# Narrower tiles toward the end, and the final combine moved to GpSimd, in a row-variance kernel

## The chip, the cores and the metric

The kernel runs on one core of one Trainium2 chip. The metric is the device time of one execution in microseconds (us). A kernel's *span* in the profile is 1.7 to 1.9 us shorter than the measured time of the same execution; I call that difference "outside".

## The reference

For each of 32 x 512 rows of 1024 floats: the mean of the squares minus the square of the mean.

```python
x = np.random.randn(32, 512, 1024).astype(np.float32)
mean_sq = np.mean(x**2, axis=-1)
sq_mean = np.mean(x, axis=-1)**2
return (mean_sq - sq_mean).astype(np.float32)
```

It reads 67 MB and writes 64 KB. The 16384 rows lie on 128 partitions, so each partition holds 128 rows. I call row *c* of all partitions together a *column*: 128 x 1024 floats, 0.5 MB.

## The kernel before

It loads 16 tiles of 8 columns (4 MB each) into 4 buffers. In each tile one column goes to the variance instructions of VectorE ("bn"), the other seven are *split*: VectorE sums them in one reduction, ScalarE squares them one by one and accumulates the sum of squares. Then ScalarE squares the mean (`mean_sq`), and VectorE does the final subtraction.

```python
io_pool = tile_pool(name="io", bufs=4);  as_pool = tile_pool(name="ascratch", bufs=2)
NBN = 1;  NSPLIT = 7                      # RPP = 8 columns per tile
for n in range(ntiles):                   # 16
    x_tile = io_pool.tile([P, RPP, D], fp32)
    nc.sync.dma_start(out=x_tile, in_=x_all[n])
    # ... bn_stats, bn_stats, bn_aggr of column 0; GpSimd copies its variance into res_all
    nc.vector.reduce_sum(out=sum_x, in_=x_tile[:, NBN:RPP, :], axis=X)
    act_scratch = as_pool.tile([P, D], fp32)          # one scratch per tile
    for j in range(NSPLIT):
        nc.scalar.activation(out=act_scratch, in_=x_tile[:, NBN + j, :],
                             func=SQ, accum_out=sum_sq[:, j : j + 1])
    nc.scalar.activation(out=mean_sq, in_=sum_x, func=SQ, scale=inv_d)
    nc.vector.scalar_tensor_tensor(out=res_all[...], in0=sum_sq, scalar=inv_d,
                                   in1=mean_sq, op0=mult, op1=subtract)
nc.sync.dma_start(out=out_v, in_=res_all)
```

## Time and profile before

| | before |
|---|---|
| measured time, median | 173.24 us (173.32 with the later runs) |
| span | 171.7 us (of an execution that took 173.46) |
| first tile taken up / last tile taken up | 13.53 / 159.93 us |
| last result written / output transfer issued | 169.18 / 169.25 us |

From the page of the kernel before: busy time of each engine, then the span in 40 slices, each digit the busy share in tenths.

```profile
DVE 145.4 (85%) x80; ACT 133.3 (78%) x241; POOL 3.2 (2%) x20
...
DVE  0008989898998989898998989899897989899893
ACT  2008969696988969696987969697895969698792
...
DMA  6999999999999999999999999999999999997000
```

The DMA row is full until slice 36, partly busy in slice 37 and then empty, while VectorE (DVE) and ScalarE (ACT) work on for three slices. That is the exposed end. The windows view of the kernel before gives, for two stretches, the length, the busy time of VectorE, ScalarE and GpSimd (POOL) with the number of instructions, the TensorE clock (not used here), the DMA share and the rate in GB/s:

```profile
20.00:80.00 60.00, 56.21 (x31) 51.15 (x94) 1.11 (x6) 1.00 1.00 432
138.00:156.00 18.00, 16.75 (x11) 15.13 (x28) 0.37 (x2) 1.00 1.00 430
```

The DMA engines are busy all the time at 430 to 432 GB/s: the load stream sets the pace, 1.22 us per column. The timeline of the kernel before, last tile (start, length, engine, line, operation, and in brackets the idle time before it and what ended it):

```profile
159.93 1.06 ACT L70 ACTIVATE act_scratch<-x_tile 128x1024 f32<-128x1024 f32 x1 [0.65 <-DMA x_tile<-in_x_dram]
159.93 0.70 DVE L55 BATCH_NORM_STATS2 stats<-x_tile 128x6 f32<-128x512 f32 x1 [0.45 <-DMA x_tile<-in_x_dram]
...
161.10 1.06 ACT L70 ACTIVATE act_scratch<-x_tile 128x1024 f32<-128x1024 f32 x1
161.13 7.60 DVE L63 TENSOR_REDUCE sum_x<-x_tile 128x7 f32<-128x7168 f32 x1
...
168.76 0.21 ACT L78 ACTIVATE mean_sq<-sum_x 128x7 f32<-128x7 f32 x1 [0.61 <-DVE sum_x L63]
...
169.01 0.17 DVE L80 SCALAR_TENSOR_TENSOR res_all<-sum_sq,mean_sq 128x7 f32<-128x7 f32 x1 [0.16 <-ACT mean_sq L78]
169.25 0.35 SPq L89 DMA_DIRECT2D out_dram<-res_all  x1
```

Nothing of the 9.25 us from 159.93 to 169.18 overlaps with loading. Note the starts of ScalarE's squares, 159.93 and 161.10. Within a tile all 96 such distances in this trace are 1.17 to 1.19 us, mostly 1.18.

### The profile page before, as it was taken

To read this page: it belongs to the slowest core of one execution; us is meant where nothing else is said; L and a number is where in the kernel's file an instruction comes from. 1 tells how busy PE (TensorE), PEld (TensorE's weight loads), DVE (VectorE), ACT (ScalarE), POOL (GpSimd) and SP (SyncE) were. 2 spreads that over 40 slices of the span, in tenths; PEclk is the share of its full clock that TensorE was granted. 3 is DMA by queue.
4 is the path that set the end of the run, shared out by engine and by line. 5 is a ranking of instruction groups with operands and counts; after the bars stand their busy time and mean duration, and the time that the engine had idled before them with its cause. 6 is when DMAs were issued, how large, how long until landed. Compare 5 with 4: busy or idle time off the path is not lost.

```text
span 171.7 us, 425 instructions
## 1 busy us (share of the span) xinstructions
DVE 145.4 (85%) x80; ACT 133.3 (78%) x241; POOL 3.2 (2%) x20
## 2 busy tenths in 40 slices
DVE  0008989898998989898998989899897989899893
ACT  2008969696988969696987969697895969698792
POOL 0000000000000000000000000000000000000000
DMA  6999999999999999999999999999999999997000
GB/s 199 428 435 428 450 420 443 443 420 443 414 435 420 443 435 435 428 443 443 412 443 420 435 428 435 420 443 437 420 437 435 428 435 435 428 428 321 0 0 15
DMA packets 2451, 67.20 MB, mean 391 GB/s; under 512 B 272, under 2 KB 400, under 8 KB 400
## 3 DMA queue, kind: packets, MB, share of 16 engines
q1 hardware_dynamic: 2448, 67.18, 91.4%
q14 instruction: 3, 0.02, 0.0%
HBM read 67.11 MB, written 0.07 MB: 391 GB/s over the span
## 4 chain that ended last, share of the span: by engine, by line
DMA 76%; DVE 21%; SPq 1%; issue 0%; ACT 0%
DMA x_tile<-in_x_dram 76%; DVE sum_x L63 18%; DVE stats L55 2%; DVE stats L56 1%; SPq L48 1%; ACT mean_sq L78 0%; DVE res_all L80 0%
## 5 line engine op out<-in xcount | busy, mean ns | idle before, releaser
L70 ACT ACTIVATE act_scratch<-x_tile 128x1024 f32<-128x1024 f32 x112 | 118.3, 1056 | 25.2 <-DMA x_tile<-in_x_dram 22.2
L63 DVE TENSOR_REDUCE sum_x<-x_tile 128x7 f32<-128x7168 f32 x16 | 121.6, 7601 | 0.0
L55 DVE BATCH_NORM_STATS2 stats<-x_tile 128x6 f32<-128x512 f32 x16 | 11.1, 694 | 21.2 <-DMA x_tile<-in_x_dram 21.2
L70 ACT ACTIVATION_READ_ACCUMULATOR act_scratch<-x_tile 128x1 f32 x112 | 20.8, 186 | 0.0
L78 ACT ACTIVATE mean_sq<-sum_x 128x7 f32<-128x7 f32 x16 | 3.3, 208 | 9.7 <-DVE sum_x L63 9.7
L56 DVE BATCH_NORM_STATS2 stats<-x_tile 128x6 f32<-128x512 f32 x16 | 10.8, 676 | 0.0
L58 POOL COPY res_all<-mv 128x1 f32<-128x1 f32 x16 | 3.0, 185 | 165.7 <-DVE mv L57 165.7
L80 DVE SCALAR_TENSOR_TENSOR res_all<-sum_sq,mean_sq 128x7 f32<-128x7 f32 x16 | 2.7, 167 | 2.5 <-ACT mean_sq L78 2.5
L57 DVE BATCH_NORM_AGGREGATE mv<-stats 128x2 f32<-128x12 f32 x16 | 3.2, 198 | 0.0
L70 ACT ACT_TABLE_LOAD x1 | 1.3, 1283 | 0.7 <-PEq L104 0.7
L104 POOL MEMSET const-float32-0.0<- 128x1 f32 x1 | 0.1, 99 | 0.2 <-issue 0.2
L104 POOL MEMSET const-bfloat16-1.0<- 128x1 bf16 x1 | 0.1, 102 | 0.0
L104 POOL MEMSET const-uint8-127<- 128x1 uint8 x1 | 0.1, 102 | 0.0
L104 POOL MEMSET const-float32-1.0<- 128x1 f32 x1 | 0.1, 99 | 0.0
## 6 DMA issues: line engine op xcount, KB each, us to landing
x_tile<-in_x_dram SPq DMA_DIRECT2D x16, 4096.0 KB, 30.0
out_dram<-res_all SPq DMA_DIRECT2D x1, 64.0 KB, 1.6
```

The lines of the kernel that those rows point to most:

```text
L48: nc.sync.dma_start(out=x_tile, in_=x_all[n])
L55: nc.vector.bn_stats(out=stats[:, j, 0], in_=x_tile[:, j, 0 : D // 2])
L56: nc.vector.bn_stats(out=stats[:, j, 1], in_=x_tile[:, j, D // 2 : D])
L57: nc.vector.bn_aggr(out=mv[:, j], in_=stats[:, j])
L58: nc.gpsimd.tensor_copy(out=res_all[:, c0 + j : c0 + j + 1], in_=mv[:, j, 1:2])
L63: nc.vector.reduce_sum(out=sum_x, in_=x_tile[:, NBN:RPP, :], axis=mybir.AxisListType.X)
L70: nc.scalar.activation(out=act_scratch, in_=x_tile[:, NBN + j, :], func=SQ, accum_out=sum_sq[:, j : j + 1],)
L78: nc.scalar.activation(out=mean_sq, in_=sum_x, func=SQ, scale=inv_d)
L80: nc.vector.scalar_tensor_tensor(out=res_all[:, c0 + NBN : c0 + RPP], in0=sum_sq, scalar=inv_d, in1=mean_sq, op0=mybir.AluOpType.mult, op1 ...
L104: nc = _bacc.Bacc("TRN2", target_bir_lowering=False, num_devices=1)
```

## The change

The intent is to shorten the exposed end. The tiles become narrow: eight of 8 columns, eleven of 4, nine of 2, two of 1. The combine goes to GpSimd in three small operations. There are five load buffers instead of four, three scratches for the squares instead of two, six buffers for the small tiles (sums, squares, results between) instead of four, and four of the 8-column tiles take two bn columns, while six of the 4-column tiles and all narrower ones take none. The diff is shortened.

```diff
-    RPP = 8; ntiles = N // (P * RPP); NBN = 1
+    sched = []
+    for i in range(4):
+        sched += [(8, 2), (8, 1)]                 # (columns, bn columns)
+    for i in range(5):
+        sched += [(4, 0), (4, 1)]
+    sched += [(4, 0)] + [(2, 0)] * 9 + [(1, 0)] * 2
-    io_pool bufs=4;  ascratch bufs=2;  small bufs=4
+    io_pool bufs=5;  ascratch bufs=3;  small bufs=6
     ...
+                    scale=inv_sqrt_d,             # in the square: msq is the mean of squares
-        nc.scalar.activation(out=mean_sq, in_=sum_x, func=SQ, scale=inv_d)
-        nc.vector.scalar_tensor_tensor(out=res_all[...], in0=sum_sq, scalar=inv_d,
-                                       in1=mean_sq, op0=mult, op1=subtract)
+            nc.gpsimd.tensor_tensor(out=t, in0=sum_x, in1=sum_x, op=mult)
+            nc.gpsimd.tensor_scalar(out=t2, in0=t, scalar1=inv_d2, op0=mult)
+            nc.gpsimd.tensor_tensor(out=res_all[...], in0=msq, in1=t2, op=subtract)
```

More of the change, by code (lines that the diff above doesn't have):

```diff
@@ L22 @@
     N = B * S
-    RPP = 8
-    W = RPP * D
-    ntiles = N // (P * RPP)
     C = N // P
     inv_d = 1.0 / D
-    x_all = x.rearrange("b s d -> (b s d)").rearrange(
-        "(p n w) -> n p w", p=P, n=ntiles, w=W
-    )
+    inv_d2 = inv_d * inv_d
+    inv_sqrt_d = float(D) ** -0.5
+    sched = []
[4 more added lines that the diff above has]
+    sched += [(4, 0)] + [(2, 0)] * 9 + [(1, 0)] * 2
+    assert sum(w for w, _ in sched) == C
+    x_cols = x.rearrange("b s d -> (b s d)").rearrange("(p c d) -> p c d", p=P, c=C)
     out_v = out.rearrange("b s -> (b s)").rearrange("(p c) -> p c", p=P)
-    io_pool = ctx.enter_context(tc.tile_pool(name="io", bufs=4))
-    as_pool = ctx.enter_context(tc.tile_pool(name="ascratch", bufs=2))
-    small = ctx.enter_context(tc.tile_pool(name="small", bufs=4))
+    io_pool = ctx.enter_context(tc.tile_pool(name="io", bufs=5))
+    as_pool = ctx.enter_context(tc.tile_pool(name="ascratch", bufs=3))
+    small = ctx.enter_context(tc.tile_pool(name="small", bufs=6))
     res_pool = ctx.enter_context(tc.tile_pool(name="res", bufs=1))
@@ L42 @@
     SQ = mybir.ActivationFunctionType.Square
-    NBN = 1
-    NSPLIT = RPP - NBN
-    for n in range(ntiles):
-        x_tile = io_pool.tile([P, RPP, D], fp32)
-        nc.sync.dma_start(out=x_tile, in_=x_all[n])
-        c0 = n * RPP
-        stats = small.tile([P, NBN, 2, 6], fp32)
-        mv = small.tile([P, NBN, 2], fp32)
-        for j in range(NBN):
-            nc.vector.bn_stats(out=stats[:, j, 0], in_=x_tile[:, j, 0 : D // 2])
-            nc.vector.bn_stats(out=stats[:, j, 1], in_=x_tile[:, j, D // 2 : D])
-            nc.vector.bn_aggr(out=mv[:, j], in_=stats[:, j])
+    MAXW = max(w for w, _ in sched)
@@ new lines @@
+    flush_after = {128: (0, 128)}
+    c0 = 0
+    for n, (w, nbn) in enumerate(sched):
+        x_tile = io_pool.tile([P, MAXW, D], fp32, name="x_tile")
+        nc.sync.dma_start(out=x_tile[:, :w, :], in_=x_cols[:, c0 : c0 + w, :])
+        nsplit = w - nbn
+        if nbn:
+            stats = small.tile([P, 2, 2, 6], fp32, name="stats")
+            mv = small.tile([P, 2, 2], fp32, name="mv")
+            for j in range(nbn):
+                nc.vector.bn_stats(out=stats[:, j, 0], in_=x_tile[:, j, 0 : D // 2])
+                nc.vector.bn_stats(out=stats[:, j, 1], in_=x_tile[:, j, D // 2 : D])
+                nc.vector.bn_aggr(out=mv[:, j], in_=stats[:, j])
@@ L58 @@
             nc.gpsimd.tensor_copy(
-                out=res_all[:, c0 + j : c0 + j + 1], in_=mv[:, j, 1:2]
+                out=res_all[:, c0 : c0 + nbn], in_=mv[:, 0:nbn, 1]
             )
-        sum_x = small.tile([P, NSPLIT], fp32)
-        nc.vector.reduce_sum(
-            out=sum_x, in_=x_tile[:, NBN:RPP, :], axis=mybir.AxisListType.X
-        )
-        sum_sq = small.tile([P, NSPLIT], fp32)
-        act_scratch = as_pool.tile([P, D], fp32)
-        for j in range(NSPLIT):
-            nc.scalar.activation(
-                out=act_scratch,
-                in_=x_tile[:, NBN + j, :],
-                func=SQ,
-                accum_out=sum_sq[:, j : j + 1],
-            )
@@ L77 @@
-        mean_sq = small.tile([P, NSPLIT], fp32)
-        nc.scalar.activation(out=mean_sq, in_=sum_x, func=SQ, scale=inv_d)
-        nc.vector.scalar_tensor_tensor(
-            out=res_all[:, c0 + NBN : c0 + RPP],
-            in0=sum_sq,
-            scalar=inv_d,
-            in1=mean_sq,
-            op0=mybir.AluOpType.mult,
-            op1=mybir.AluOpType.subtract,
-        )
-    nc.sync.dma_start(out=out_v, in_=res_all)
+        if nsplit:
+            sum_x = small.tile([P, MAXW], fp32, name="sum_x")
+            nc.vector.reduce_sum(
+                out=sum_x[:, :nsplit],
+                in_=x_tile[:, nbn:w, :],
+                axis=mybir.AxisListType.X,
+            )
+            msq = small.tile([P, MAXW], fp32, name="msq")
+            act_scratch = as_pool.tile([P, D], fp32)
+            for j in range(nsplit):
+                nc.scalar.activation(
+                    out=act_scratch,
+                    in_=x_tile[:, nbn + j, :],
+                    func=SQ,
+                    scale=inv_sqrt_d,
+                    accum_out=msq[:, j : j + 1],
+                )
+            t = small.tile([P, MAXW], fp32, name="t")
+            nc.gpsimd.tensor_tensor(
+                out=t[:, :nsplit],
+                in0=sum_x[:, :nsplit],
+                in1=sum_x[:, :nsplit],
+                op=mybir.AluOpType.mult,
+            )
+            t2 = small.tile([P, MAXW], fp32, name="t2")
+            nc.gpsimd.tensor_scalar(
+                out=t2[:, :nsplit],
+                in0=t[:, :nsplit],
+                scalar1=inv_d2,
+                scalar2=None,
+                op0=mybir.AluOpType.mult,
+            )
+            nc.gpsimd.tensor_tensor(
+                out=res_all[:, c0 + nbn : c0 + w],
+                in0=msq[:, :nsplit],
+                in1=t2[:, :nsplit],
+                op=mybir.AluOpType.subtract,
+            )
@@ L93 @@
+        c0 += w
+        if c0 in flush_after:
+            lo, hi = flush_after[c0]
+            nc.sync.dma_start(out=out_v[:, lo:hi], in_=res_all[:, lo:hi])
 _INS = ['x']
```

## The prediction

> **What bounds it now.** The load stream. The windows view shows the DMA engines 100% busy at 430 to 433 GB/s from 20 to 140 us. The Trainium skill ("DMA: Bandwidth & Descriptors", Specifications) gives 435 GB/s as the fabric ceiling; the trace agrees. Tiles of eight columns (4 MB) land every 9.71 us typically, 9.76 on average: 1.22 us per column. VectorE (85% busy) and ScalarE (78%) wait for each tile. Exposed is the end: the timeline shows the last tile starting at 159.93; its work ends at 169.18, 9.25 us later, and the output transfer ends the span at 171.7 (2.5 us). The measured 173.24 is 1.5 above the span.
>
> **What changes.** The same bytes in 30 loads instead of 16: eight of 8 columns, eleven of 4, nine of 2, two of 1. The combine moves to GpSimd; `mean_sq` leaves ScalarE. ScalarE takes 116 squares instead of 112, none skipped in the last 24 columns.
>
> **Costs, from the trace.** A ScalarE square starts every 1.18 us (1.056 plus the accumulator read). A reduced VectorE column is 7.60/7 = 1.09 us, a bn column about 1.2. GpSimd's 128x1 copy took 0.185 us; I estimate 0.2 to 0.3 for each of its three small operations. 4 MB at 435 GB/s would be 9.64 us against 9.71, so a load's own overhead is some 0.08 us (estimate): 14 more loads add 1 us of stream.
>
> **The naive gain** is: last load lands near 161, then 1.25 us for one square, 0.3 for the subtract, 2.5 output, 1.5 outside: 166.5.
>
> **I expect less, because ScalarE arrives late.** In the last 24 columns it squares every column at 1.18 us against 1.22 to 1.26 for arrival, so it hardly gains on the stream. When the last 4-column tile lands (column 108: 13.5 + 100 x 1.22 + 0.5 = 136.0) it has a 4.7 us block to do while the following 2-column tile lands after 2.5 us. That lag of over 2 us then shrinks by only about 0.1 us per tile. ScalarE ends at 136.0 + 24 x 1.18 = 164.3, some 3.3 us after the last landing instead of 1.25. Adding 0.3 for the subtract and 2.5 for the output: span 167.1, time 168.7. VectorE at 1.09 per column catches up by the last tiles and does not matter. Five buffers suffice: the lag is two small tiles.
>
> **Predicted: 168.7 us, range 167.2 to 170.3.** Faster by over 2% (below 169.8): 0.78; within 2%: 0.21; slower: 0.01.
>
> **What would show it right.** The DMA row stays at nines until about 160 with 420 GB/s or more in the narrow tiles. In the last 28 us ScalarE has no idle gaps, back to back at 1.18 us, with loads landed before it asks. The chain of waits ends with output, GpSimd subtract, a run of ScalarE squares of about 28 us, and before that DMA. VectorE waits for DMA at the end, ScalarE does not.
>
> **What would make it wrong.**
> - Narrow rows (8 KB and 4 KB per partition instead of 32 KB) stream more slowly: then the last landing moves past about 163 and DMA, not ScalarE, ends the chain; slower, up to 170 or more.
> - The late buffers come free too late: the DMA row dips in the last 25 us and the queue waits for ScalarE.
> - GpSimd's operations take far longer than 0.3 us each: its queue backs up, and the final subtract is late by as much.
> - The lag disappears, if squares of different tiles overlap better than 1.18 us: nearer 167.

## The result

The changed kernel takes 167.97 us (8 runs, 167.94 to 168.07) against 173.32: ratio 0.9692, 95% interval 0.9682 to 0.9702. Executions over 1.5% slower than the fastest of the same kernel are left out of the means. A ratio here is the mean time of one kernel's runs over that of the other's of the same rounds, so not quite the ratio of the medians. The predicted 168.7 (167.2 to 170.3) holds. The path to it does not hold in every step. It had ScalarE's squares, back to back for 28 us, at the end of the chain that ends last; the trace has a wait for a load there, then VectorE and GpSimd.

From the page of the changed kernel:

```profile
DVE 143.3 (86%) x81; ACT 127.1 (76%) x223; POOL 20.5 (12%) x107
...
DVE  0007989899897989989899999999999999999991
ACT  3007849695796939879399999886987969999991
POOL 0000010100101010010101111111111111322232
DMA  6999999999999999999999999999999999999930
```

The span is 166.2 us. The DMA row is now full almost to the end. The windows view of the changed kernel, same stretches as before:

```profile
20.00:80.00 60.00, 55.74 (x34) 45.17 (x80) 4.64 (x24) 1.00 1.00 430
138.00:156.00 18.00, 17.63 (x9) 17.63 (x33) 4.45 (x22) 1.00 1.01 422
```

The 2-column loads run at 422 GB/s, not 430: a small price. The timeline of the changed kernel from 143 us, ScalarE only, in the 2-column tiles:

```profile
143.33 1.06 ACT L81 ACTIVATE act_scratch<-x_tile 128x1024 f32<-128x1024 f32 x1
...
144.39 1.04 ACT L81 ACTIVATE act_scratch<-x_tile 128x1024 f32<-128x1024 f32 x1
...
145.55 1.06 ACT L81 ACTIVATE act_scratch<-x_tile 128x1024 f32<-128x1024 f32 x1
...
146.61 1.04 ACT L81 ACTIVATE act_scratch<-x_tile 128x1024 f32<-128x1024 f32 x1
```

The starts are 1.06, 1.16 and 1.06 us apart. The longer distance is that between the two squares of one tile, which write the same scratch; the shorter is that to the next tile, which writes another. I read this as a wait: the square that goes to the scratch which the previous square has just written waits for it. Experiments e3 and e4 test it. So ScalarE needs 2.22 us for two columns, not 2.36. In the whole trace 77 of 81 squares start 1.16 to 1.19 us after the one before them in their tile; the other four, where the tiles become narrower, start after 1.04 to 1.05, and why is not shown (the trace leaves out which buffer a square writes). The end of the same timeline, with VectorE, GpSimd and the output:

```profile
155.87 1.06 ACT L81 ACTIVATE act_scratch<-x_tile 128x1024 f32<-128x1024 f32 x1 [0.17 <-DMA x_tile<-in_x_dram]
...
158.35 1.06 ACT L81 ACTIVATE act_scratch<-x_tile 128x1024 f32<-128x1024 f32 x1
158.36 4.54 DVE L72 TENSOR_REDUCE sum_x<-x_tile 128x2 f32<-128x2048 f32 x3 [0.19 <-DMA x_tile<-in_x_dram]
...
161.62 1.04 ACT L81 ACTIVATE act_scratch<-x_tile 128x1024 f32<-128x1024 f32 x1
...
162.98 0.19 POOL L90 TENSOR_TENSOR t<-sum_x 128x1 f32<-128x1 f32 x1 [0.35 <-DVE sum_x L72]
163.26 0.21 POOL L97 TENSOR_SCALAR t<-t 128x1 f32<-128x1 f32 x1
163.56 0.19 POOL L104 TENSOR_TENSOR res_all<-msq,t 128x1 f32<-128x1 f32 x1
163.77 0.35 SPq L114 DMA_DIRECT2D out_dram<-res_all  x1
```

ScalarE waits for a load again at 155.87: it has caught up with the stream. When the last 2-column tile lands, near 158.3, both engines start on it at once, and the two last columns land behind it while they work. VectorE ends at 162.90, ScalarE at 162.76 (its last accumulator read, the 0.19 us instruction that follows every square in the trace), and then GpSimd's three operations follow on VectorE's sum and end at 163.75. The last result is written 5.4 us earlier than before (169.18), which is the gain. Its two parts can be worked out from the landing times that the packed trace keeps: the last load lands at 160.77 instead of 159.90, which costs 0.9 us, and the last result follows 3.0 us later instead of 9.3, which gains 6.3.

### The profile page after: what moved, and what is told of

Its sections match the earlier page's. It is cut to its first block, busy times and chain, and to the rows that moved or that the text cites. A ratio compares the mean times of both kernels' runs of the same rounds, so it can differ in the third digit from the quotient of the medians.

```text
span 166.2 us, 584 instructions
## 1 busy us (share of the span) xinstructions
DVE 143.3 (86%) x81; ACT 127.1 (76%) x223; POOL 20.5 (12%) x107
## 4 chain that ended last, share of the span: by engine, by line
DMA 72%; DVE 12%; ACT 7%; issue 5%; DVEq 1%; SPq 1%; POOL 0%; POOLq 0%; ACTq 0%
DMA x_tile<-in_x_dram 72%; DVE sum_x L72 10%; ACT act_scratch L81 7%; DVEq L140 1%; DVE stats L63 1%; SPq L55 1%; DVE stats L64 1%; POOL t L90 0%; POOLq L140 0%; POOL t L97 0%; DVE mv L65 0%; POOL res_all L66 0%; DVEq L72 0%; POOLq L104 0%; ACTq L81 0%
## 5 line engine op out<-in xcount | busy, mean ns | idle before, releaser
L81 ACT ACTIVATE act_scratch<-x_tile 128x1024 f32<-128x1024 f32 x111 | 117.0, 1054 | 35.0 <-DMA x_tile<-in_x_dram 27.0
L72 DVE TENSOR_REDUCE sum_x<-x_tile 128x2 f32<-128x2048 f32 (+5 forms) x30 | 121.8, 4082 | 1.1 <-DMA x_tile<-in_x_dram 0.6
L63 DVE BATCH_NORM_STATS2 stats<-x_tile 128x6 f32<-128x512 f32 x17 | 11.7, 688 | 18.6 <-DMA x_tile<-in_x_dram 18.6
L90 POOL TENSOR_TENSOR t<-sum_x 128x2 f32<-128x2 f32 (+5 forms) x30 | 5.9, 196 | 137.3 <-DVE sum_x L72 137.3
L64 DVE BATCH_NORM_STATS2 stats<-x_tile 128x6 f32<-128x512 f32 x17 | 11.3, 667 | 0.0
L97 POOL TENSOR_SCALAR t<-t 128x2 f32<-128x2 f32 (+5 forms) x30 | 6.9, 228 | 2.6
L104 POOL TENSOR_TENSOR res_all<-msq,t 128x2 f32<-128x2 f32 (+5 forms) x30 | 5.9, 196 | 3.1 <-ACT act_scratch L81 0.7
L66 POOL COPY res_all<-mv 128x1 f32<-128x1 f32 (+1 forms) x13 | 2.4, 185 | 0.0
```

What stands on the lines that cost most here:

```text
L63: nc.vector.bn_stats(out=stats[:, j, 0], in_=x_tile[:, j, 0 : D // 2])
L64: nc.vector.bn_stats(out=stats[:, j, 1], in_=x_tile[:, j, D // 2 : D])
L66: nc.gpsimd.tensor_copy(out=res_all[:, c0 : c0 + nbn], in_=mv[:, 0:nbn, 1])
L72: nc.vector.reduce_sum(out=sum_x[:, :nsplit], in_=x_tile[:, nbn:w, :], axis=mybir.AxisListType.X,)
L81: nc.scalar.activation(out=act_scratch, in_=x_tile[:, nbn + j, :], func=SQ, scale=inv_sqrt_d, accum_out=msq[:, j : j + 1],)
L90: nc.gpsimd.tensor_tensor(out=t[:, :nsplit], in0=sum_x[:, :nsplit], in1=sum_x[:, :nsplit], op=mybir.AluOpType.mult,)
```

## The experiments

Twelve kernels ran, all correct, each beside the kernel before on the same chip. Except the control, each changes what its (shortened) diff shows; e7 and e9 rewrite the work on a tile, so several things change there at once. Two of the change's parts were not varied alone: the six buffers for small tiles, and the bn columns, which go with the tiles. Two questions stood: which part of the change brings the gain, and what ends the changed kernel.

### The old combine in the new tiles (e1)

```diff
-            three GpSimd operations (t, t2, subtract)
+            nc.scalar.activation(out=mean_sq, in_=sum_x, func=SQ, scale=inv_d)
+            nc.vector.scalar_tensor_tensor(out=res_all[...], in0=msq, scalar=1.0,
+                                           in1=mean_sq, op0=mult, op1=subtract)
```

> The new tiles and new bn share, but the old combine: mean_sq on ScalarE after sum_x, final subtract on VectorE. Theory A (the gain is the small last tiles alone): about 168, within 0.3 of the changed kernel. Theory B (the combine on GpSimd is what lets the engines keep up with narrow tiles, because with the old one each engine waits for the other once per tile): a 2-column tile costs VectorE about 2.2 + 0.2 + 0.2 of work and some 0.1 of handing over, 2.7 us against an arrival every 2.5, so the lag grows in the tail: 170 to 172 us, and VectorE shows waits for mean_sq in the last 25 us.

Measured: 172.52 us, ratio 0.9959 (0.9944 to 0.9974). Narrow tiles and five buffers without the GpSimd combine gain 0.7 us of 5.4. From the timeline of this kernel, one 2-column tile and the start of the next (ScalarE's squares left out):

```profile
149.77 0.20 ACT L90 ACTIVATE mean_sq<-sum_x 128x2 f32<-128x2 f32 x1 [0.20 <-DVE sum_x L72]
...
150.01 0.16 DVE L93 SCALAR_TENSOR_TENSOR res_all<-msq,mean_sq 128x2 f32<-128x2 f32 x1 [0.27 <-ACT mean_sq L90]
150.09 2.28 DVE L72 TENSOR_REDUCE sum_x<-x_tile 128x2 f32<-128x2048 f32 x1
...
152.40 0.20 ACT L90 ACTIVATE mean_sq<-sum_x 128x2 f32<-128x2 f32 x1 [0.20 <-DVE sum_x L72]
```

The two engines go in lockstep: ScalarE waits for VectorE's sum, VectorE then waits for ScalarE's small square. The period is 152.40 - 149.77 = 2.63 us, and a 2-column tile arrives every 2.5. The engines are slower than the stream, so the lag grows through the 2-column tiles. Of the 2.63 us VectorE is idle for 0.27; without that wait it would need about 2.36 (an estimate), less than 2.5. So it is the waiting, and not the moved work alone, that makes the tile too slow. The lag holds up the stream too: the last load lands at 161.98, 1.2 us later than in the changed kernel. Theory B holds, a little beyond its range.

### The old tiles with the new combine (e2, and e11 with four buffers)

```diff
-    sched = (the taper)
+    sched = [(8, 1)] * 16
-    io_pool bufs=5        # e11 only
+    io_pool bufs=4        # e11 only
```

> The combine on GpSimd, five buffers and three scratches, but the sixteen tiles of 8 columns with one bn column each. Theory A (the new combine frees time by itself): 170 to 172. Theory B (it only matters together with narrow tiles; the stream sets the pace and the last tile still needs its 7.6 us reduction, then three GpSimd operations of 0.77 us in all instead of 0.4 for the old combine): 173.3 to 173.9.

Measured: 174.59 us (174.16 to 175.51), ratio 1.0048 (1.0018 to 1.0079). So the combine alone brings nothing; it costs, more than theory B allowed. The profile fell on the slowest of these runs, 175.51, and shows four of fifteen tile spacings at 10.0 to 10.6 us, where 9.7 is usual and the kernel before has one such (10.19). (The next expectation says six against two; by the starts of the bn instructions it is four against one.) I suspected the fifth buffer.

> The sixteen 8-column tiles with the combine on GpSimd, now with the four load buffers of the kernel before. With five it took 174.6, over my 173.3 to 173.9, because six of its fifteen tile spacings were 10.0 to 10.6 us instead of 9.7, against two in the kernel before. Theory A (five 4 MB loads queued at once disturb the stream): spacings as before, 173.3 to 173.7. Theory B (irregular spacings that have nothing to do with the buffers): 174 to 175 again, or anything between.

Measured: 173.94 us (173.89 to 173.96), ratio 1.0035 (1.0021 to 1.0048). The last tile was taken up at 159.88, as in the kernel before, and what is left, 0.6 us, is about the longer GpSimd combine at the end, as expected. But the intervals of the two ratios overlap, and the kernel before itself was a little slower and less steady beside e2 (173.47 against 173.31), so an effect of the fifth buffer on this kernel is not shown. Why 4 MB loads are now and then over 10 us apart stays open.

### One scratch for the squares (e3), and one for each square in turn (e4)

```diff
-    as_pool = tile_pool(name="ascratch", bufs=3)                     # e3
+    as_pool = tile_pool(name="ascratch", bufs=1)
-            act_scratch = as_pool.tile([P, D], fp32)                 # e4
             for j in range(nsplit):
+                act_scratch = as_pool.tile([P, D], fp32, name="act_scratch")
```

> The changed kernel with one scratch buffer for the squares instead of three. Theory A (my forecast was 0.7 us too high because squares that go to another scratch buffer start after 1.05 us, and only those to the same buffer after 1.18): now all start every 1.18 us, the 24 last squares take 28.3 us from about 135.6, ScalarE ends near 164.0 instead of 162.8, and the time is 168.6 to 168.9. Theory B (the late end is VectorE's and GpSimd's, ScalarE has slack): unchanged, 167.9 to 168.1.

Measured: 169.56 us, ratio 0.9787 (0.9772 to 0.9801). The end of its timeline, ScalarE's last squares:

```profile
161.35 1.06 ACT L81 ACTIVATE act_scratch<-x_tile 128x1024 f32<-128x1024 f32 x1
...
162.58 1.06 ACT L81 ACTIVATE act_scratch<-x_tile 128x1024 f32<-128x1024 f32 x1
...
163.81 1.06 ACT L81 ACTIVATE act_scratch<-x_tile 128x1024 f32<-128x1024 f32 x1
```

Now squares start every 1.18 us within a tile and every 1.23 across tiles. The last 24 run from 136.12 to 164.97 (the last accumulator read) without a wait for a load, and ScalarE ends the kernel. This is the picture that I had predicted. It is 0.7 us slower than theory A's upper end: ScalarE ends 1.0 us later than expected there, 0.55 of it from eleven distances of 1.23 that I had not foreseen, and 0.5 because the 24 squares began at 136.12 and not at 135.6.

> The changed kernel with a scratch buffer of its own for each square in turn (three rotating). Every square should then start after 1.05 us. Theory A (ScalarE ends the kernel): up to 1 us faster, 167.0 to 167.4. Theory B (VectorE's last reductions, then three small GpSimd operations, end it): within 0.1 of 167.97.

Measured: 168.33 us (168.20 to 168.45), ratio 0.9715 (0.9700 to 0.9729). From its timeline, two late squares and VectorE's last reductions:

```profile
147.73 1.04 ACT L81 ACTIVATE act_scratch<-x_tile 128x1024 f32<-128x1024 f32 x1
...
148.77 1.04 ACT L81 ACTIVATE act_scratch<-x_tile 128x1024 f32<-128x1024 f32 x1
...
158.53 4.54 DVE L72 TENSOR_REDUCE sum_x<-x_tile 128x2 f32<-128x2048 f32 x3 [0.22 <-DMA x_tile<-in_x_dram]
```

All 81 squares that follow another in their tile now start after 1.03 to 1.06 us, against 1.18 to 1.19 with one scratch: the scratch makes the difference. ScalarE waits for loads in the last tiles. Theory A falls: a faster ScalarE gains nothing. VectorE again does its three last reductions in one run of 4.54 us, from 158.53. To see whether this kernel is truly slower than the changed one, that one ran again, unchanged, as a control:

> The changed kernel itself again, as a control for these runs and for the ones before (the one with a scratch buffer per square came out 0.36 us slower than it): 167.9 to 168.1 if that difference was the kernel's, up to 168.4 if it was the chip's.

Measured: 168.20 us (167.99 to 168.56), ratio 0.9691 (0.9664 to 0.9718). The intervals overlap, so no difference between the two is shown.

### A short taper (e5)

```diff
-    sched = (the taper of the change)
+    sched = [(8, 1)] * 15 + [(4, 0), (2, 0), (1, 0), (1, 0)]
```

> Fifteen tiles of 8 columns, then 4, 2, 1, 1, with the new combine. Theory A (the end is set by the size of the last tile): like the changed kernel or better, since 19 loads cost less than 30: 167 to 168. Theory B (the engines run at some 90% of the stream's time per column, so a lag from a wide tile is worked off by only 0.1 us per column and the taper must begin early): the last 8-column tile lands near 150.1, VectorE needs 8.9 us for it and then 8.9 us for the 8 columns behind it, ending near 167.9; time 172 to 173.

Measured: 173.21 us, ratio 0.9996 (0.9979 to 1.0012). The same last tile of one column, and no gain at all. From its timeline:

```profile
150.21 0.69 DVE L58 BATCH_NORM_STATS2 stats<-x_tile 128x6 f32<-128x512 f32 x1 [0.79 <-DMA x_tile<-in_x_dram]
...
159.05 8.81 DVE L67 TENSOR_REDUCE sum_x<-x_tile 128x4 f32<-128x4096 f32 x4
...
168.52 0.19 POOL L99 TENSOR_TENSOR res_all<-msq,t 128x1 f32<-128x1 f32 x1
```

The last 8-column tile is taken up at 150.21 and occupies VectorE until 159; on the 8 columns behind it, VectorE works 8.8 us without waiting for a load once, to 167.86. VectorE needs about 1.1 us per split column and the stream brings one every 1.22, so a lag of one wide tile shrinks by some 0.1 us per column. It takes tens of columns to work off. The change narrows its tiles from column 64 on, which leaves room for that.

### Only 2-column tiles (e6)

```diff
-    sched = (the taper of the change);  io_pool bufs=5
+    sched = [(2, 0)] * 64;              io_pool bufs=20
```

> 64 tiles of 2 columns, no bn, twenty buffers: no taper at all, and the lag of a wide tile never arises. What it measures is the cost of a load: in the changed kernel the stream ran at 432 GB/s with 8 columns and 422 with 2, so 64 loads take 159.0 us instead of 155.4. Theory B (that cost is 0.06 us per 1 MB load): last landing near 163, then 2.2 + 0.8 + 2.5 + 1.7: 169.5 to 170.5. Theory A (loads of this size cost nothing extra, and small tiles all along are as good as a taper): 167.5 to 168.

Measured: 170.87 us, ratio 0.9841 (0.9818 to 0.9865). The windows view and the last reduction in the timeline of this kernel:

```profile
20.00:150.00 130.00, 118.49 (x53) 119.04 (x209) 31.40 (x156) 1.00 1.01 422
```

```profile
163.28 2.29 DVE L67 TENSOR_REDUCE sum_x<-x_tile 128x2 f32<-128x2048 f32 x1 [0.17 <-DMA x_tile<-in_x_dram]
```

With 64 loads the last tile lands at 163.3 instead of 159.9 with 16: 3.4 us for 48 more loads, 0.07 us each. There is no lag: from the last landing to the last result it is 3.1 us (163.28 to 166.4) instead of 9.25. The time is 0.4 us above theory B's range. Of these 6.1 us the loads' own cost takes back 3.4. So in this kernel a taper is the right form: wide tiles while the end is far, narrow ones only as far back as the lag needs.

### Four load buffers (e8)

```diff
-    io_pool = tile_pool(name="io", bufs=5)
+    io_pool = tile_pool(name="io", bufs=4)
```

> The changed kernel with four load buffers instead of five. Theory A (the fifth buffer carries the lag of the narrow tiles): 0.5 us or more slower, the DMA row dips in the last 25 us. Theory B (a lag of at most two small tiles leaves loads queued with four as well): within 0.2 of the changed kernel's 167.97 to 168.2, ratio to the kernel before 0.968 to 0.971.

Measured: 169.64 us, ratio 0.9786 (0.9767 to 0.9804): 1.4 us slower than the control, 1.7 slower than the first runs with five. From its windows view:

```profile
138.00:156.00 18.00, 16.86 (x8) 16.87 (x31) 4.26 (x21) 1.00 0.95 386
```

The stream falls from 422 to 386 GB/s in this stretch; the hole lies between 142 and 144 us, where the windows view shows 156 GB/s. The last load lands at 162.58 instead of 160.77, and these 1.8 us are the whole loss of the profiled run (169.87). My reading of the hole: a buffer is as large as an 8-column tile whatever it holds, and while the engines finish their last 4-column tile, three queued 2-column loads last only 3 x 2.5 = 7.5 us. That the fifth buffer prevents the hole is shown, this working is not. Theory A holds: the fifth buffer pays.

### The last combine on VectorE (e10)

```diff
+            if n == len(sched) - 1:      # two operations instead of three on GpSimd
+                nc.vector.scalar_tensor_tensor(out=t, in0=sum_x, scalar=inv_d2, in1=sum_x, op0=mult, op1=mult)
+                nc.vector.tensor_tensor(out=res_all[...], in0=msq, in1=t, op=subtract)
```

> The changed kernel, but the last tile's combine is two VectorE operations instead of three on GpSimd. In the changed kernel GpSimd starts 0.08 us after VectorE's last reduction and its three operations end 0.77 us later, on the chain that ends last. Two VectorE operations took about 0.43 us from the end of the reduction to the result in the whole-column kernel, with ScalarE's square in between. Theory A (GpSimd's three operations are on the critical path at the end): 0.3 to 0.4 us faster than the changed kernel, ratio to the kernel before about 0.967. Theory B (they hide behind ScalarE's last square): no change, 0.969 to 0.970.

Measured: 167.84 us (167.72 to 167.94), ratio 0.9682 (0.9669 to 0.9695). From its timeline:

```profile
158.44 4.54 DVE L72 TENSOR_REDUCE sum_x<-x_tile 128x2 f32<-128x2048 f32 x3 [0.21 <-DMA x_tile<-in_x_dram]
...
163.36 0.16 DVE L99 TENSOR_TENSOR res_all<-msq,t 128x1 f32<-128x1 f32 x1
163.59 0.35 SPq L131 DMA_DIRECT2D out_dram<-res_all  x1
```

In this profile the output transfer is issued at 163.59 instead of 163.77, though its last 2-column tile landed 0.08 us later. So GpSimd's operations were on the path, worth some 0.26 us in the profile; in the timed runs the gain is 0.1 to 0.2, less than theory A said, and not clear of the changed kernel's interval.

### Whole columns for each engine (e7, e9): a version that beats both

A split column costs VectorE 1.09 and ScalarE 1.04 to 1.18 us, 2.2 engine-microseconds. A bn column costs VectorE some 1.4 us and ScalarE nothing. A square and a copy, both with accumulated sums, cost ScalarE 2.1 us and VectorE nothing. Dealing whole columns to both engines needs some 0.85 us per column instead of 1.1 (an estimate from these durations).

```diff
+    # e7: columns in the tile: (bn on VectorE, whole on ScalarE, split)
+    MIX = {8: (5, 3, 0), 4: (2, 1, 1), 2: (1, 1, 0), 1: (0, 0, 1)}
+    sched = [8] * 13 + [4] * 4 + [2] * 3 + [1] * 2
+            nc.scalar.activation(out=s2, in_=x_tile[:, nb + j, :], func=Copy,
+                                 accum_out=sum_x[:, j : j + 1])
     # a new scratch for every square and copy
     # last tile: combine on VectorE, as above
-    # e9: [2] * 3 + [1] * 2
+    [2] * 2, then four single columns: bn, whole on ScalarE, bn, split
```

> An attempt to beat both: most columns are done whole by one engine, bn on VectorE (about 1.4 us a column) or square and copy with accumulated sums on ScalarE (2.1 us), so the two together need some 0.85 us per column against 1.22 for the stream, not 1.1; the lag is worked off three times as fast and the taper can be shorter: 8x13, 4x4, 2x3, 1x2, 22 loads instead of 30. The last column is split, and its combine is two VectorE operations. If the lag theory is right: last landing near 159.8, ScalarE and VectorE end within 1.3 us of it, combine 0.35, output 2.5, outside 1.7: 165.3 to 166.3. If the engines' lag was not what held the changed kernel: no better than 167.5.

Measured: 167.34 us, ratio 0.9641 (0.9616 to 0.9666). Faster, but not in the expected range of 165.3 to 166.3: the engines had caught up by 131 us, and then, as I read the timeline, the last 2-column tile gave ScalarE a column of 2.1 us just before the end. Dealing, schedule and last combine change together here, so the gain is not assigned to one of them.

> The whole-column kernel with another end. In it both engines waited for the stream from 131 us on, but the last 2-column tile, landed at 158.4, gave ScalarE a whole column of 2.1 us with two single squares behind it, so it ended at 162.7, some 2 us after the last landing. Here the last four columns are single tiles that go in turn to VectorE (bn), ScalarE (square and copy), VectorE (bn), and both (split), so each engine should be free when its column lands. Theory A (what is left at the end is work assigned to a busy engine): about 0.6 us faster than the whole-column kernel, 166.5 to 167.0, ratio to the kernel before about 0.962. Theory B (the stream's end or fixed costs set it): no change, 167.2 to 167.5.

Measured: 167.02 us (166.90 to 167.18), ratio 0.9636 (0.9624 to 0.9648). Its interval lies below that of the changed kernel (0.9682 to 0.9702): 0.6% faster, and the lowest ratio of all, just above its expected range. It overlaps with that of e7, so that the other end helps is not shown. From its timeline:

```profile
160.84 1.06 ACT L79 ACTIVATE act_scratch<-x_tile 128x1024 f32<-128x1024 f32 x1 [0.28 <-POOL t L114]
...
161.04 1.20 DVE L72 TENSOR_REDUCE sum_x<-x_tile 128x1 f32<-128x1024 f32 x1
...
162.61 0.16 DVE L107 TENSOR_TENSOR res_all<-msq,t 128x1 f32<-128x1 f32 x1
162.84 0.35 SPq L137 DMA_DIRECT2D out_dram<-res_all  x1
```

ScalarE stood idle before the last column; the view names a GpSimd operation on another tile as its release, but the square also needs its load. The trace settles it: the last load was issued at 156.21 and landed 4.5 us later (the shortest time to landing in its tile view), at 160.73, 0.11 us before the square. From 160.84 the result takes 1.9 us. What is left is one column's work, the output and the fixed parts. In its last stretch (155 to 158 us) the stream ran at 354 GB/s; probably five buffers with single columns in them hold too little, but no run tests it.

### All runs together

| kernel | time, us | ratio to before |
|---|---|---|
| changed | 167.97 | 0.9692 |
| changed, again (control) | 168.20 | 0.9691 |
| old combine (e1) | 172.52 | 0.9959 |
| old tiles (e2) / with four buffers (e11) | 174.59 / 173.94 | 1.0048 / 1.0035 |
| one scratch (e3) / one per square (e4) | 169.56 / 168.33 | 0.9787 / 0.9715 |
| short taper (e5) | 173.21 | 0.9996 |
| only 2-column tiles (e6) | 170.87 | 0.9841 |
| four buffers (e8) | 169.64 | 0.9786 |
| last combine on VectorE (e10) | 167.84 | 0.9682 |
| whole columns (e7) / with another end (e9) | 167.34 / 167.02 | 0.9641 / 0.9636 |

The parts do not add up: taking out the new combine loses 4.6 us, taking out the tiles 6.6 (6.0 with four buffers), and the whole gain is 5.4. The combine gains nothing without the tiles, and the tiles little without the combine.

## Why the prediction was right or wrong

- **The bound and the exposed end: right.** The stream sets the pace, and the gain is the end's shrinking. Shown by the traces, and by e5 and e6, which change the tiles and with them the bn columns (15 and none instead of 17; e6 has more buffers too).
- **The cost of 14 more loads, 1 us: right in size.** e6 gives 0.07 us per load against my estimate of 0.08.
- **A lag that a narrow last tile does not cure: right as a mechanism.** e5 shows it on VectorE to the tenth of a microsecond (167.9 expected, 167.86 measured).
- **"A ScalarE square starts every 1.18 us": mis-sized, and the step that failed.** I read 1.18 from a kernel where nearly every square writes the scratch of the square before. In the changed kernel a square into a new scratch starts after 1.04 to 1.06. The Trainium skill ("ScalarE: Activation LUTs", What ACT_TABLE_LOAD costs) states 186 ns plus 0.833 ns per element for an ACTIVATE with immediate scale and bias, which gives an estimate of 1.04 us at 1024 elements, and that back-to-back ones overlap by about 93 ns. The trace's durations of 1.04 to 1.06 us agree with the first; with the second it agrees where no wait stands between, for there a square and its accumulator read (0.19 us) together go every 1.04 us. A second square into the same scratch loses the overlap (1.18 us), as e3 and e4 show from both sides. So the 24 last squares ended at 162.76, not 164.3 (1.2 us of this by the shorter distances, 0.4 because they began at 135.64 and not at 136.0), and ScalarE's lag was gone by 155.87. The prediction had named this itself among what would make it wrong ("if squares of different tiles overlap better than 1.18 us"). e3, with one scratch, restores the predicted picture (and 169.56 us).
- **"VectorE catches up by the last tiles and does not matter": wrong in its second half.** It caught up (it waits for loads at 153.4, 155.9 and 158.4), but it ended last. e4 shows that ScalarE did not hold the end.
- **"0.3 for the subtract", and GpSimd's first two operations done before the square: wrong at the one tile that counts.** There VectorE's sum came after the square, so all three operations stood on the path: 0.85 us from 162.90 to 163.75. e10 shows a part of that as a gain.
- **"Five buffers suffice": right;** e8 shows that four do not.
- **The combine: undervalued.** I named the move to GpSimd and costed it, but did not see that with the old combine the two engines would run in lockstep slower than the stream (e1). The sum was right without it because the change has the combine moved.
- **A slip:** I counted 116 squares; with 17 bn columns there are 111 (128 - 17). It touches no step, as the last 24 columns were counted right.

The total was 0.7 us too high. The engines' end was put 1.4 us too late (164.3 instead of VectorE's 162.90), and two errors of the other sign made up half of it: the combine took 0.85 us and not 0.3, and 1.8 us lay outside and not 1.5. The 1.5 was no measurement of one execution: it set the median time, 173.24, against the span of an execution that took 173.46. That the total came so close is in part luck.

## What to carry to other kernels

In a stream-bound kernel like this one, the exposed end is not only the last tile's work but the lag of the slowest engine, and that shrinks only by the difference between the stream's time per unit and the engine's (here 1.22 - 1.1 us per column); compute that difference before choosing where to begin a taper. Narrow tiles need engines that do not wait for each other once per tile: a tiny combine on an idle engine, off both busy queues, can be what makes them pay. Scratch outputs that nobody reads still ordered the instructions that wrote them (a square every 1.18 us instead of 1.04); rotate them when the engine is near its limit.

## What the Trainium skill lacked or had wrong

- "GPSIMD Engine Reference", Engine selection, says to use VectorE and not GpSimd for elementwise work. For operations of 1 to 7 elements per partition the runs show 0.19 to 0.26 us each on GpSimd and about 0.16 on VectorE, and leaving them off VectorE and ScalarE was worth 4.6 us (e1): for tiny work in this kernel the queue that it blocked counted, not the rate.
- "ScalarE: Activation LUTs", What ACT_TABLE_LOAD costs, gives the overlap of back-to-back ACTIVATEs, but not that writing the previous one's output buffer removes it: 1.04 us against 1.18 (1.23 across tiles with one scratch for all) at 128x1024 with an accumulated sum. It also has no figure for the accumulator read, 0.19 us in the profile.
- "DMA: Bandwidth & Descriptors", Measured, lists 341 GB/s for a 1 MB transfer issued from GpSimd, and its Rules ask for 1 MiB and more. For loads queued behind each other from the sync engine the runs give 432 GB/s at 4 MB, 425 at 2 MB and 422 at 1 MB, or 0.07 us of own cost per load (e6). The page has no table by size for loads queued from the sync engine (a single rate of such a stream stands in its part on iDMA).
- "Perfetto Trace Analysis" does not speak of lag; its section Optimizing Scalar/DVE Operations says that, where ScalarE and VectorE are not saturated but hold up other engines, breaking up instructions may allow work to be completed sooner. Here narrow tiles gained over a long stretch (167.97 us with the taper, 170.87 with 2-column tiles throughout, against 173.3 to 173.5); a short taper gained nothing (173.21 against 173.26).
- No page tells why equal 4 MB loads, mostly 9.7 us apart, are now and then 10.0 to 10.6 us apart; the runs do not either.
